# Layer A's attention: output-projection pairs prepared behind the last scores, and gate weights fetched for six products at a time

## The chip, the core and the metric

The kernel runs on one core of a Trainium2 chip. The metric is device microseconds (us) of one execution; lower is better. The time quoted for the kernel before is the median of three runs. Durations of single instructions come from one further execution, taken by the hardware profiler.

## What is computed

A two-layer decoder trunk over 2048 tokens, model width 1024, in float32. Only the first layer, layer A, matters here:

```python
u = rmsnorm(h, norm_a_g[i])
proj = u @ w_in_a[i]
q, k, v, f_logit, gate = jnp.split(proj, [...], axis=-1)
...
o = fox_attention(q, k, v, log_f).reshape(b, s, WIDTH_A)
h = h + (o * jax.nn.silu(gate)) @ w_out_a[i]
```

There are 16 heads of 64 dimensions. `fox_attention` is causal softmax attention whose logits carry a cumulative log forget gate. Layer B (sliding-window attention over shared keys and values) follows and is not touched.

## The kernel before, in words

Every float32 matrix product is made of three products of a high and a low part (high x high, high x low, low x high), so operands are first split: ScalarE (ACT) copies the rounded high part, and VectorE (DVE) or GpSimd (POOL) subtracts it from the original to get the low part.

`attention_a` runs 320 steps: 16 heads, for each four chunks of 512 queries, for each chunk 2, 4, 6 or 8 steps of two 128-key blocks. In a step, TensorE (PE) makes the scores (L975, L976), ACT takes the exponential (L990) and the high part (L993), POOL subtracts for the low part (L994), DVE adds the weights into the running row sums in PSUM (L1003), and three steps later PE multiplies with V (L1018). Beside this, "pieces" for the next head find the row maxima: PE at L927, DVE at L938 and L943, and four small copies per 512 queries (L554) on SyncE's queue (SP). At the end of a chunk DVE folds the sums (L888).

The silu gate's projection, 768 products in 32 units of 24 (L1052), is spread between the steps as filler. For each unit, the weights come in tiles of 512 KB that serve twelve products (L1048), from two buffers with the tag `wr`. The last 48 of the 768 products are kept for after the last scores, when the softmax values still have to come: there the tiles alternate between buffers `st` (four, which held the exponentials) and `wr`. A finished unit goes through DVE, ACT, DVE (L1059 to L1061) and is stored.

The output projection `out_a` then runs over 32 pairs, four chunks of 512 tokens by eight pairs of heads, 24 products a pair (L1221). A pair is loaded by `Pairs.load`: two halves of the attention output, the gate, and reciprocal sums (`gated_load`, five transfers into four 256 KB tiles, L1169 to L1174). `Pairs.prepare` then makes it ready (`gated`): POOL adds the halves (L1184), DVE multiplies by the reciprocals and by the gate (L1185, L1186), ACT copies the high part (L1187), DVE subtracts for the low part (L1188). The first pairs are loaded and prepared inside `attention_a` at steps 284 and 298 (`PREP_AT`), and the load of a third follows the last step. In `out_a`, step `s` loads ahead to pair `s + 5`, prepares pair `s + 2`, splits the output weight of pair `s + 2` (`weight_split`, L131 and L132) and loads that of pair `s + 4` into an `st` buffer (L122).

The order in which an engine gets its instructions is not the program's own: a planner orders them by priority (program order) and by when it reckons that operands and buffers are ready, so that early-ready work may be issued well before the place where it is written. `keep_in_program_order` places an instruction behind the one traced before it on its engine. All transfers here are issued on SP's one queue, in order. At run time each engine takes its instructions strictly in the order so fixed, and waits where an operand is missing.

Of the kernel before, what the change touches and what calls it, by code (L numbers as in the profile page):

```python
# [13 lines left out]
F32R = mybir.dt.float32r  # L14
# [3 lines left out]
ALU = mybir.AluOpType  # L18
# [4 lines left out]
P = 128  # L23
# [3 lines left out]
NDT = D // P  # L27
# [4 lines left out]
CH = 512  # L32
# [9 lines left out]
SUM_LAG = 5  # L42
LOAD_AT = 7

PREP_AT = (284, 298)

RAW_AT = 302

# [44 lines left out]
def f_(ap):  # L93
    return ap.bitcast(F32)


class Pairs:
# [6 lines left out]
        self.loaded = self.ready = 0  # L104

    def load(self, s, tags=("wh", "wl", "wh", "wl")):
        self.tiles[s] = [self.t.sb(tag, [P, CH]) for tag in tags]
        self.t.gated_load(s // NDT, s % NDT, self.tiles[s])
        self.loaded = s + 1

    def prepare(self, s):
        if s % 4 == 0:
            self.Y[s // 4] = self.t.sb("big", [P, 4, 2, CH], F32R)
        self.t.gated(self.y(s), self.tiles.pop(s))
        self.ready = s + 1

    def y(self, s):
# [28 lines left out]
class Trunk:  # L146
# [693 lines left out]
    def attention_a(self, op):  # L840


        nc, tc, d = self.nc, self.tc, self.d
        kbt, qbt = self.sb("big", [P, 2, S], F32R), self.sb("big", [P, 2, S], F32R)
        for i in range(2):
# [6 lines left out]
            out=mask_m[:, -P:], in_=mask_m[:, -P:], pattern=[[-1, P]], compare_op=ALU.is_ge,  # L852
# [40 lines left out]
        def recips(h, c0=0, c1=NCH):  # L893

            nr = (c1 - c0) * NSB
            ps = self.ps("sc", [nr, 32])
            nc.tensor.matmul(
                ps, part[:, h % 2, c0:c1].rearrange("p c b -> p (c b)"), self.fold,
                start=True, stop=True,
            )  # L900
            rc = self.sb("sq", [nr, 32])
            nc.vector.tensor_tensor(rc, ps, roots[:nr, 1 if c0 else 0], ALU.mult)
            nc.vector.reciprocal(rc, rc)
            nc.sync.dma_start(
                out=d["rd"][h, c0 * CH : c1 * CH].rearrange("(b i) -> b i", i=32), in_=rc
            )
# [101 lines left out]
        def values(item):  # L1008
            u, p, ph, pl = item
            h, ch = units[u]  # L1010
            v = heads[h][4]
            if p == 0:
                state[u][1] = self.ps("pa", [P, CH])
            pv = state[u][1]
            last = p == 2 * ch + 1
            for n_, (k, q0, w, off) in enumerate(blocks(ch, p)):
                for i, src in enumerate((ph, pl)):
                    nc.tensor.matmul(  # L1018
                        pv[:, q0 : q0 + w], v[:, k, :], src[:, off : off + w],
                        start=(p == 0 and n_ == 0 and i == 0),  # L1020
                        stop=(last and n_ == 1 and i == 1),
                    )
            if last:
                state.pop(u)
                ov = self.sb("sq", [P, CH])
                nc.scalar.copy(ov, pv)  # L1026
                rows, cols = slice(h * HD, (h + 1) * HD), slice(ch * CH, (ch + 1) * CH)
                nc.sync.dma_start(out=d["om"][rows, cols], in_=ov[:HD, :])
                nc.sync.dma_start(out=d["oc"][rows, cols], in_=ov[HD:, :])

        def gate():


            for ch in range(NCH):
                rows, us = self.factor_rows(0, ch), []
                for dt in range(NDT):
                    us.append([self.sb(t, [P, CH], F32R) for t in ("wh", "wl")])
                    for k in range(2):
                        nc.sync.dma_start(out=f_(us[dt][k]), in_=d["ut"][ch, k, dt])
                for ft in range(NDT):  # L1040
                    if gate_bank == "mx":
                        ps = self.ps("mx", [P, 2, CH])[:, 0]
                    else:
                        ps = self.ps(gate_bank, [P, CH])
                    for dt in range(NDT):
                        if dt % 4 == 0:
                            w = self.sb(next(weight_slots), [P, 2, 2, 2, P], F32R)
                            nc.sync.dma_start(  # L1048
                                out=f_(w), in_=d["wg"][ft, :, dt // 2 : dt // 2 + 2]
                            )  # L1050
                        for i, (wk, uk) in enumerate(((0, 0), (0, 1), (1, 0))):
                            nc.tensor.matmul(  # L1052
                                ps, w[:, dt // 2 % 2, wk, dt % 2, :], us[dt][uk],
                                start=(dt == 0 and i == 0), stop=(dt == NDT - 1 and i == 2),
                            )
                            if dt < NDT - 1 or i < 2:
                                yield
                    g = self.sb("sq", [P, CH])
                    nc.vector.tensor_tensor(g, ps, rows, ALU.mult)  # L1059
                    nc.scalar.activation(g, g, AF.Tanh, scale=0.5)  # L1060
                    nc.vector.scalar_tensor_tensor(g, g, 1.0, ps, ALU.add, ALU.mult)  # L1061
                    nc.sync.dma_start(
                        out=d["gt"][ft * P : (ft + 1) * P, ch * CH : (ch + 1) * CH], in_=g
                    )
                    yield

        pieces, done, loaded = [], 0, 0

        def more_pieces(n):
            nonlocal loaded  # L1070
            while len(pieces) < n and loaded < H:
                load_max(loaded)
                if loaded:
                    load_rest(loaded)
                for ch in range(NCH):
                    pieces.extend(max_pieces(loaded, ch))
                loaded += 1
# [8 lines left out]
        def ahead(target):  # L1086
            nonlocal done
            while done < min(target, len(pieces)):
                pieces[done]()
                done += 1  # L1090
# [6 lines left out]
        yield  # L1097
        pht, plt = self.sb("big", [P, 4, 1024], F32R), self.sb("big", [P, 4, 1024], F32R)
        filler, fed, total = gate(), 0, NCH * NDT * NDT * 3
        gate_bank, weight_slots, rest = "pb", cycle(["wr"]), False  # L1100

        def feed(n, pause=False):


            nonlocal fed, rest
            if pause and rest:
                rest = False
                return
            while fed < min(total, n):
                next(filler, None)  # L1110
                fed += 1
                if pause and fed % (3 * NDT) == 0:
                    rest = True
                    break
# [3 lines left out]
        for n, (u, p) in enumerate(steps):  # L1118
            h, ch = units[u]
            if n % per_head == LOAD_AT and h + 1 < H:  # L1120
                more_pieces(len(pieces) + 1)
            target = per * (n + AHEAD + 1) // per_head + 1
            ahead(target - 1)
            pending.append(scores(n, u, p))
            ahead(target)
            if len(pending) > V_LAG:
                values(pending.pop(0))
            if p == 2 * ch + 1:
                if h == H - 1 and ch in (0, NCH - 1):
                    due.append((n + SUM_LAG, (h, ch and 1, ch + 1)))  # L1130
                elif ch == NCH - 1:
                    due.append((n + SUM_LAG, (h,)))
            while due and due[0][0] <= n:
                recips(*due.pop(0)[1])
            feed((total - KEPT) * (n + 1) // len(steps), pause=True)
            if n == RAW_AT:
                raw = self.sb("big", [P, NDT // 2, D])
                for p in range(NDT // 2):
                    op.weight_load(p, raw[:, p])
            if n in PREP_AT:  # L1140
                op.load(PREP_AT.index(n), ("qn", "wh", "qn", "wl"))
                op.prepare(PREP_AT.index(n))
        op.load(2, ("qn", "wh", "qn", "wl"))
        gate_bank, weight_slots = "mx", cycle(["st", "wr"])
        for item in pending:
            values(item)
            feed(fed + NDT)
        gate_bank = "pb"
        for _, args in due:
            recips(*args)  # L1150
        for p in range(PAIRS_READY):
            op.weight_split(p)
        for _ in filler:
            pass

# [20 lines left out]
                in_=d["rd"][h : h + 1, cols].to_broadcast([HD, CH]),  # L1176
            )

    def gated(self, y, tiles):

        nc = self.nc
        m, c, g, rb = tiles
        yh, yl = (y[:, k] for k in range(2))
        nc.gpsimd.tensor_tensor(m, m, c, ALU.add)  # L1184
        nc.vector.tensor_tensor(m, m, rb, ALU.mult)  # L1185
        nc.vector.tensor_tensor(m, m, g, ALU.mult)  # L1186
        nc.scalar.copy(yh, m)  # L1187
        nc.vector.tensor_tensor(yl, m, f_(yh), ALU.subtract)  # L1188
# [50 lines left out]
    def attention_b(self, w_out, res, dst):  # L1239
# [117 lines left out]
        W = [None, self.half(w_out, 1)]  # L1357
        msg, php, yt = self.sb("big", [P, 4, 1024]), None, None
        load(0)
        load_v(0)  # L1360
        yield
# [176 lines left out]
```

## Time and profile before

| | |
|---|---|
| median of three runs | 2511.83 us (2511.45 to 2513.24) |
| the profiled execution's own time | 2508.55 us |
| its span, first to last instruction | 2506.8 us |
| PE busy | 2455.1 us, 98% of the span |
| DVE busy | 1766.5 us, 70% |
| ACT busy | 1332.5 us, 53% |
| POOL busy | 919.8 us, 37% |
| DMA | 419.30 MB, mean 167 GB/s |

Layer A's attention runs from 594 us, the first scores, to 1484.73 us, the first product of the output projection. Times in rows are microseconds from the span's start. A "busy" PE is not one at its peak: a matrix product counts from its start to its modelled end, and consecutive ones overlap, so PE's rate is better read from how many products a stretch holds and from the granted clock. A bracket at the end of a timeline row gives the engine's idle time just before it and what ended that.

### The profile page before, as it was taken

The page shows a single profiled execution, that of the slowest core. Times are in us where ns is not written, and L with a number is a line of the kernel's source. Part 1 is how long each engine was busy: PE and PEld are TensorE (multiplying, and loading weights), DVE is VectorE, ACT ScalarE, POOL GpSimd, SP SyncE. Part 2 cuts the span into 40 slices and gives each one's busy share as a digit, 9 for nine tenths or more (in the row PEclk, how much of TensorE's full clock was granted, in tenths as well). Part 3 has the DMA queues.
Part 4 walks back from the last instruction along what each step waited for, and adds up shares of the span by engine and source line. Part 5 has one row for each costly group of instructions (what it writes and reads, how often), then busy time and mean ns, then how long its engine had stood idle before and what let it go on. Part 6 is the DMA issues. An engine that isn't in the chain of part 4 may idle for free. (4 is left out here: it accounts for less than half of the span.)

```text
span 2506.8 us, 37302 instructions
## 1 busy us (share of the span) xinstructions
PE 2455.1 (98%) x12256; PEld 2050.1 (82%) x12256; DVE 1766.5 (70%) x4255; ACT 1332.5 (53%) x2574; POOL 919.8 (37%) x611
## 2 busy tenths in 40 slices
PE   8999999999999999999999999999999999899999
PEld 6788899988888777877877778888788888688887
DVE  7656666726888888888888965556666323788885
ACT  5423333415777777877777751145332214777774
POOL 0000000014777777777777752200011000455542
PEclk9999999999999999999999999999999999999999
DMA  5656645687555655565466469965443424755551
GB/s 181 204 158 190 178 148 151 199 268 222 141 149 151 201 142 158 150 186 160 123 202 161 144 186 282 283 216 159 114 131 84 141 91 141 206 168 158 160 143 64
DMA packets 351521, 419.30 MB, mean 167 GB/s; under 512 B 64928, under 2 KB 248256, under 8 KB 345152
## 3 DMA queue, kind: packets, MB, share of 16 engines
q1 hardware_dynamic: 351328, 416.92, 57.3%
q8 instruction: 97, 1.59, 0.3%
q14 instruction: 96, 0.79, 0.1%
HBM read 265.29 MB, written 151.40 MB: 166 GB/s over the span
## 5 line engine op out<-in xcount | busy, mean ns | idle before, releaser
L750 PE MATMUL b<-wh,big 128*128 128x512 f32 (+3 forms) x2560 | 771.6, 375 | 9.2 <-ACT wh L480 8.8
L994 POOL TENSOR_TENSOR big<-st,big 128x1024 fp32r<-128x1024 f32 (+1 forms) x320 | 659.2, 2075 | 276.0 <-ACT big L993 172.0
L750 PEld LDWEIGHTS b<-wh,big 128*128 128x128 f32 x2560 | 472.3, 189 | 80.2 <-ACT wh L480 11.4
L750 PE MATMUL b<-wl,big 128*128 128x512 f32 (+3 forms) x1280 | 474.4, 371 | 1.6 <-DVE wl L481 1.6
L1003 DVE TENSOR_TENSOR ac<-ac,st 128x512 f32<-128x512 f32 (+3 forms) x576 | 355.1, 617 | 53.2 <-ACT st L990 24.5
L990 ACT ACTIVATE st<-sc 128x512 f32<-128x512 f32 (+1 forms) x512 | 274.9, 584 | 158.6 <-PE sc L976 82.5
L1018 PE MATMUL pa<-big 128*128 128x512 f32 (+3 forms) x1280 | 327.1, 370 | 3.2 <-POOL big L994 1.1
L993 ACT CAST big<-st 128x1024 fp32r<-128x1024 f32 (+1 forms) x320 | 295.6, 924 | 7.9
L750 PEld LDWEIGHTS b<-wl,big 128*128 128x128 f32 x1280 | 242.0, 189 | 38.0 <-DVE wl L481 5.5
L1018 PEld LDWEIGHTS pa<-big 128*128 128x128 f32 x1280 | 223.0, 190 | 49.3 <-ACT sq L1026 16.8
L489 ACT ACTIVATE sq<-b,r 128x512 f32<-128x512 f32 (+2 forms) x128 | 77.8, 608 | 302.4 <-PE b L750 299.2
L938 DVE CUSTOM_DVE_ANT_0 mx<-mx,rot 128x128 f32<-128x128 f32 (+3 forms) x240 | 210.5, 877 | 39.3 <-PE mx L927 31.0
L975 PE MATMUL sc<-big 128*128 128x512 f32 (+3 forms) x640 | 231.1, 365 | 1.3 <-DVE st L536 1.1
L976 PE MATMUL sc<-big 67*128 67x512 f32 (+3 forms) x640 | 229.9, 368 | 0.0
L927 PE MATMUL mx<-big 66*128 66x128 f32 (+3 forms) x660 | 192.1, 365 | 11.2 <-DVE mt L938 10.6
L1052 PE MATMUL pb<-wh,wr 128*128 128x512 f32 x488 | 179.3, 399 | 3.8 <-DMA wr<-wg 3.2
L491 DVE TENSOR_REDUCE sm<-sq 128x8 f32<-128x512 f32 (+2 forms) x128 | 74.9, 585 | 139.3 <-ACT sq L489 139.0
L715 PE MATMUL b<-big,wh 128*128 128x512 f32 x512 | 158.3, 390 | 1.4 <-DVE st L721 1.3
L1309 POOL TENSOR_TENSOR st<-st,rs 128x1024 f32<-128x1024 f32 (+1 forms) x64 | 118.4, 1850 | 109.9 <-DVE rs L1308 101.8
L850 POOL MEMSET rot<- 128x1024 bf16 x1 | 1.0, 952 | 421.0 <-PE pb L343 421.0
L927 PEld LDWEIGHTS mx<-big 66*128 66x128 f32 x660 | 113.7, 191 | 50.9 <-DVE mt L938 20.9
L975 PEld LDWEIGHTS sc<-big 128*128 128x128 f32 x640 | 121.6, 190 | 23.1 <-DVE st L536 1.5
(252 smaller groups left out, 4306.4 us busy)
## 6 DMA issues: line engine op xcount, KB each, us to landing
wr<-wg SPq DMA_DIRECT2D x62, 512.0 KB
va<-st SPq DMA_DIRECT2D x32, 512.0 KB
ka<-st SPq DMA_DIRECT2D x64, 256.0 KB
ut<-big SPq DMA_DIRECT2D x16, 1024.0 KB
big<-ka SPq DMA_DIRECT2D x16, 1024.0 KB
big<-qa SPq DMA_DIRECT2D x16, 1024.0 KB
qb<-st SPq DMA_DIRECT2D x64, 256.0 KB
big<-qb SPq DMA_DIRECT2D x16, 1024.0 KB
```

Source lines behind the costliest of these rows:

```text
L715: nc.tensor.matmul(ps, W[k][dt][:, ft * P : (ft + 1) * P], u[ch][:, dt, :], start=(dt == 0 and i == 0), stop=(dt == NDT - 1 and i == 2),)
L750: nc.tensor.matmul(ps[:, :n], u[tb // 4][:, dt, us], W[k][dt], start=(dt == 0 and i == 0), stop=(dt == NDT - 1 and i == 2),)
L927: mm = nc.tensor.matmul(ps[:, b, :wb], qb[:66, i * P : (i + 1) * P], kb[:66, k0 + b * wb : k0 + (b + 1) * wb], start=True, stop=True,)
L938: nc.vector.tensor_tensor_reduce(out=lg, in0=lg, in1=mask, scale=1.0, scalar=NEG, op0=ALU.add, op1=ALU.max, accum_out=f_(o),)
L975: nc.tensor.matmul(o, ka[:, ks], qa[:, qs], start=not (last and n_), stop=False)
L976: nc.tensor.matmul(o, kb[:, ks], qb[:, qs], start=False, stop=not diag)
L990: nc.scalar.activation(pf[:, off : off + w], ps[:, :w], AF.Exp, scale=HD**-0.5)
L993: nc.scalar.copy(ph[:, :tw], pf[:, :tw])
L994: nc.gpsimd.tensor_tensor(pl[:, :tw], pf[:, :tw], f_(ph[:, :tw]), ALU.subtract)
L1003: nc.vector.tensor_tensor(a_, a_, pf[:, off : off + w], ALU.add)
L1018: nc.tensor.matmul(pv[:, q0 : q0 + w], v[:, k, :], src[:, off : off + w], start=(p == 0 and n_ == 0 and i == 0), stop=(last and n_ == 1 an ...
L1052: nc.tensor.matmul(ps, w[:, dt // 2 % 2, wk, dt % 2, :], us[dt][uk], start=(dt == 0 and i == 0), stop=(dt == NDT - 1 and i == 2),)
```

## The change

The pairs' first preparation leaves the score loop. At step 298 pair 0 is only loaded. Behind the last step pair 1 is loaded into two `st` buffers, pair 0 is prepared with its addition (POOL) and first multiplication (DVE) pinned in program order, and pair 2 is loaded into the buffers of pair 0. Pair 1 is prepared, pinned likewise, ahead of the last 24 gate products. The gate weights are fetched in places of 256 KB for six products: four places in the two `wr` buffers during the steps, and four more in two `st` buffers after them.

```diff
-PREP_AT = (284, 298)
+PAIR_AT = 298
...
     def load(self, s, tags=("wh", "wl", "wh", "wl")):
-        self.tiles[s] = [self.t.sb(tag, [P, CH]) for tag in tags]
+        if len(tags) == 4:
+            self.tiles[s] = [self.t.sb(tag, [P, CH]) for tag in tags]
+        else:
+            both = [self.t.sb(tag, [P, 2, CH]) for tag in tags]
+            self.tiles[s] = [t[:, k] for t in both for k in range(2)]
...
-    def prepare(self, s):
+    def prepare(self, s, pin=False):
...
-                        if dt % 4 == 0:
-                            w = self.sb(next(weight_slots), [P, 2, 2, 2, P], F32R)
-                            nc.sync.dma_start(
-                                out=f_(w), in_=d["wg"][ft, :, dt // 2 : dt // 2 + 2]
-                            )
+                        if dt % 2 == 0:
+                            w = next(weight_slots)
+                            nc.sync.dma_start(out=f_(w), in_=d["wg"][ft, :, dt // 2])
...
+        def weight_places(tag):
+            tiles = [self.sb(tag, [P, 2, 2, 2, P], F32R) for _ in range(2)]
+            return [t[:, k] for t in tiles for k in range(2)]
...
-        gate_bank, weight_slots, rest = "pb", cycle(["wr"]), False
+        places = weight_places("wr")
+        gate_bank, weight_slots, rest = "pb", cycle(places), False
...
-            if n in PREP_AT:
-                op.load(PREP_AT.index(n), ("qn", "wh", "qn", "wl"))
-                op.prepare(PREP_AT.index(n))
+            if n == PAIR_AT:
+                op.load(0, ("qn", "wh", "qn", "wl"))
+        gate_bank, weight_slots = "mx", cycle(weight_places("st") + places)
+        op.load(1, ("st", "st"))
+        op.prepare(0, pin=True)
         op.load(2, ("qn", "wh", "qn", "wl"))
-        gate_bank, weight_slots = "mx", cycle(["st", "wr"])
         for item in pending:
             values(item)
             feed(fed + NDT)
...
         for p in range(PAIRS_READY):
             op.weight_split(p)
+        feed(total - 3 * NDT)
+        op.prepare(1, pin=True)
         for _ in filler:
             pass
...
-    def gated(self, y, tiles):
+    def gated(self, y, tiles, pin):
...
-        nc.gpsimd.tensor_tensor(m, m, c, ALU.add)
-        nc.vector.tensor_tensor(m, m, rb, ALU.mult)
+        both = (
+            nc.gpsimd.tensor_tensor(m, m, c, ALU.add),
+            nc.vector.tensor_tensor(m, m, rb, ALU.mult),
+        )
+        for ins in both if pin else ():
+            self.tc.keep_in_program_order(ins)
```

## Rows read from the trace of the kernel before

**Rows 1.** Busy time by stretch, heads 10 to 14; the columns stand first.

```profile
core 0: us, PE busy (x) PEld busy (x) DVE busy (x) ACT busy (x) POOL busy (x), PEclk, DMA share, GB/s
1133.35:1188.47 55.12, 54.27 (x266) 43.59 (x265) 47.21 (x88) 41.58 (x66) 41.08 (x21) 1.00 0.54 153
1188.47:1242.67 54.20, 53.94 (x266) 43.76 (x265) 47.38 (x89) 41.26 (x66) 40.97 (x21) 1.00 0.50 128
1242.67:1300.62 57.95, 54.70 (x267) 43.93 (x266) 47.23 (x89) 41.35 (x67) 41.09 (x21) 1.00 0.67 203
1300.62:1362.96 62.34, 57.99 (x275) 46.14 (x274) 54.92 (x94) 43.72 (x70) 44.65 (x22) 0.97 0.60 158
1362.96:1423.95 60.99, 56.94 (x268) 45.05 (x267) 54.79 (x95) 43.04 (x68) 44.85 (x23) 0.97 0.51 150
```

**Rows 2.** Timeline of DVE: the fold of the sums that ends head 13.

```profile
1362.26 0.70 DVE L888 TRANSPOSE_TENSOR_REDUCE part<-ac 128x16 f32<-128x512 f32 x1
```

**Rows 3.** Timeline of POOL: first and last of four pair additions among the scores.

```profile
1335.04 1.29 POOL L1184 TENSOR_TENSOR qn<-qn,wh 128x512 f32<-128x512 f32 x1 [2.68 <-PE pa L1018]
...
1406.56 1.28 POOL L1184 TENSOR_TENSOR wh<-wh,wl 128x512 f32<-128x512 f32 x1 [1.08 <-DMA wl<-oc]
```

**Rows 4.** Groups of DVE instructions from 1335 to 1416 us; columns first.

```profile
line engine op names shapes xcount | busy us, mean ns | idle before us <-releasers
L1003 DVE TENSOR_TENSOR ac<-ac,st 128x512 f32<-128x512 f32 (+3 forms) x46 | 29.1, 632 | 2.7 <-ACT st L990 1.1 <-ACT ac L997 1.1
...
L1185 DVE TENSOR_TENSOR qn<-qn,wl 128x512 f32<-128x512 f32 x3 | 8.2, 2726 | 2.2 <-POOL qn L1184 1.3 <-DMA wl<-rd 0.8
L1188 DVE TENSOR_TENSOR big<-qn,big 128x512 fp32r<-128x512 f32 x3 | 4.2, 1404 | 0.0
```

**Rows 5.** PE's waits, 1330 to 1420 us (total, times, longest).

```profile
PE mx L927 <- DVE mt L938: 7.6, 4, 2.8
```

**Rows 6.** Timeline of PE behind one such wait: slow products, then fast.

```profile
1407.12 0.63 PE L975 MATMUL sc<-big 128*128 128x512 f32 x1
...
1410.38 0.39 PE L1052 MATMUL pb<-wh,wr 128*128 128x512 f32 x1
```

**Rows 7.** PE's waits, 590 to 1500 us: gate weights not landed.

```profile
PE pb L1052 <- DMA wr<-wg: 3.2, 5, 1.9
```

**Rows 8.** Timeline behind the last scores: POOL, DVE.

```profile
1454.61 18.28 POOL L994 TENSOR_TENSOR big<-st,big 128x1024 fp32r<-128x1024 f32 x8 [1.23 <-ACT big L993]
...
1469.17 2.86 DVE L132 TENSOR_TENSOR big<-big 128x1024 fp32r<-128x1024 f32 x1 [0.94 <-ACT big L131]
...
1473.08 1.21 DVE L132 TENSOR_TENSOR big<-big 128x1024 fp32r<-128x1024 f32 x1
1474.22 0.70 DVE L888 TRANSPOSE_TENSOR_REDUCE part<-ac 128x16 f32<-128x512 f32 x1
```

**Rows 9.** Timeline, one pair from load (SP) through POOL to ready (DVE).

```profile
1481.61 0.38 SPq L1169 DMA_DIRECT2D wh<-om  x1
...
1486.72 1.28 POOL L1184 TENSOR_TENSOR wh<-wh,wl 128x512 f32<-128x512 f32 x1 [13.84 <-DMA wh<-om]
...
1491.24 0.95 DVE L1188 TENSOR_TENSOR big<-wh,big 128x512 fp32r<-128x512 f32 x1 [0.75 <-ACT big L1187]
```

**Rows 10.** Timeline of PE: the output projection begins.

```profile
1484.73 1.52 PE L1221 MATMUL b<-big 128*128 128x512 f32 x6
1487.11 3.04 PE L1221 MATMUL b<-big 128*128 128x512 f32 x12 [0.86 <-DVE sq L1061]
```

**Rows 11.** Busy time by stretch around the seam; columns as in rows 1.

```profile
1470.00:1480.00 10.00, 8.98 (x42) 6.75 (x41) 8.67 (x12) 4.09 (x7) 2.88 (x2) 1.00 0.68 204
...
1500.00:1510.00 10.00, 10.00 (x46) 8.28 (x45) 4.67 (x6) 1.94 (x3) 2.79 (x2) 1.00 1.03 332
```

**Rows 12.** Timeline of DVE: pair 6 ready, then output weight 7 ready.

```profile
1499.44 0.69 DVE L1188 TENSOR_TENSOR big<-wh,big 128x512 fp32r<-128x512 f32 x1 [0.69 <-ACT big L1187]
...
1513.17 1.23 DVE L132 TENSOR_TENSOR big<-st,big 128x1024 fp32r<-128x1024 f32 x1 [0.26 <-ACT big L131]
```

**Rows 13.** SP's own waits, 590 to 1470 us (total, times, longest).

```profile
SPq L1048 <- PE pb L1052: 77.1, 18, 9.8
SPq L554 <- DVE ac L1003: 56.6, 61, 3.3
```

More of the change, by code (lines that the diff above doesn't have):

```diff
@@ L106, in load @@
     def load(self, s, tags=("wh", "wl", "wh", "wl")):
-        self.tiles[s] = [self.t.sb(tag, [P, CH]) for tag in tags]
+        if len(tags) == 4:
[3 more added lines that the diff above has]
+            self.tiles[s] = [t[:, k] for t in both for k in range(2)]
         self.t.gated_load(s // NDT, s % NDT, self.tiles[s])
         self.loaded = s + 1
-    def prepare(self, s):
+    def prepare(self, s, pin=False):
         if s % 4 == 0:
             self.Y[s // 4] = self.t.sb("big", [P, 4, 2, CH], F32R)
-        self.t.gated(self.y(s), self.tiles.pop(s))
+        self.t.gated(self.y(s), self.tiles.pop(s), pin)
         self.ready = s + 1
@@ L1045, in gate @@
                     for dt in range(NDT):
-                        if dt % 4 == 0:
-                            w = self.sb(next(weight_slots), [P, 2, 2, 2, P], F32R)
-                            nc.sync.dma_start(
-                                out=f_(w), in_=d["wg"][ft, :, dt // 2 : dt // 2 + 2]
-                            )
+                        if dt % 2 == 0:
+                            w = next(weight_slots)
+                            nc.sync.dma_start(out=f_(w), in_=d["wg"][ft, :, dt // 2])
                         for i, (wk, uk) in enumerate(((0, 0), (0, 1), (1, 0))):
                             nc.tensor.matmul(
-                                ps, w[:, dt // 2 % 2, wk, dt % 2, :], us[dt][uk],
+                                ps, w[:, wk, dt % 2, :], us[dt][uk],
                                 start=(dt == 0 and i == 0), stop=(dt == NDT - 1 and i == 2),
```

## The prediction

> **What bounds the kernel now.** The page comes first: PE is busy for 98% of the span, so what counts is where PE stands still or is slowed in the stretch that the change touches. I then cut layer A's attention by heads and read the busy times by stretch. The reader should see that a head has a steady price: 55.12 and 54.20 us for heads 10 and 11 [rows 1]; each stretch ends with the fold of the head's last sums, as head 13's at 1362.26 + 0.70 [rows 2]. Head 12 takes 57.95, and heads 13 and 14 take 62.34 and 60.99, with about the same number of products [rows 1]. In these last two DVE's busy time grows from 47 to 55 us, and the granted clock falls from 1.00 to 0.97 [rows 1]. So something is added to DVE there, and PE pays.
>
> The timeline of POOL says what: four pair additions stand among the scores, from 1335 to 1407 us [rows 3]. The program writes only two preparations there. The planner has moved them ahead of their place and has pulled a third pair and half of a fourth in behind them. The groups of DVE show the price. The first multiplication of a pair takes 2.73 us in the mean and the last subtraction 1.40 [rows 4], where the running sums, with one input in PSUM and mostly of the same size, keep 0.63 in the same stretch [rows 4]. Three first multiplications make 8.2 us and also kept DVE idle for 2.2 us before them [rows 4]. DVE takes its work in order, so the maxima and sums queued behind them come late, and PE waits for them four times, 7.6 us in all [rows 5]. Behind such a wait PE's products take 0.63 us instead of 0.39 for over 3 us [rows 6]: the granted clock, whose mean over these heads is 0.97 [rows 1], is at the lower of its two levels, 1.2 instead of 2.4 GHz.
>
> The last view is of the seam between the scores and the output projection, where the removed work must go; its rows come with the steps below.
>
> **The change part by part.**
>
> *Out of the score loop.* No preparation is left among the scores: pair 0 is pinned behind the last of POOL's and DVE's work for them, pair 1 behind pair 0, and pair 2 needs the buffers of pair 0. Heads 13 and 14 should then cost what heads 10 and 11 cost, 54.66 in the mean: 62.34 + 60.99 - 2 x 54.66 = 14.0 us [rows 1]. I count the waits and the slow products inside this sum, not beside it. With head 11 as the measure it would be 14.9; if only the four waits went, 7.6 [rows 5].
>
> *Gate weights in places of six.* A buffer is refilled when its last product is done. With two buffers of twelve, the next fetch has the time of twelve products to land; with four places of six, that of eighteen. PE now waits 3.2 us for such fetches in five waits, the longest 1.9 [rows 7]. Some 45 products go into a head of 54.66 us, 1.2 us each, so the lead grows by 7 us, more than the longest wait. The gain lies between nothing (if the queue ahead of a fetch, and not the free buffer, sets its time) and 3.3 us (all that head 12 takes over heads 10 and 11 [rows 1]). I take 2.0. The number of fetches doubles from 64 (two for each of 32 units) to 128 at half the size; their issue lies on SP, and its price is a rival below.
>
> *Pair 0 behind the last scores.* POOL ends its last subtraction at 1472.89 and DVE folds the last sums at 1474.22 to 1474.92 [rows 8]. The chain of a pair from POOL's addition to the last subtraction, its waits included, took 1492.19 - 1486.72 = 5.5 us [rows 9]. Pair 0, loaded long before, is so ready near 1480.4. The projection starts at 1484.73 [rows 10], under the 48 kept gate products that PE works on meanwhile. So it costs nothing, with 4.3 us of cover; without it, each us late is a us.
>
> *Pair 1.* Its two `st` buffers come free when POOL is done, 1472.9. From issue to ready the pair in [rows 9] took 1492.19 - 1481.61 = 10.6 us, so pair 1 is ready near 1483.6. PE took six products, waited, and went on at 1487.11 [rows 10]; at 46 products in 10 us [rows 11] a pair's 24 take 5.2, so the next pair starts near 1491.0. Cover 7.4 us, cost nothing. What is queued behind its pinned multiplication on DVE is the finishing of the last gate unit, for which PE waits at the start of the projection (0.86 us idle at 1487.11 [rows 10]). DVE's added instructions there are short, 0.69 each [rows 12]; one or two of them before that finishing make 0 to 1.4 us. I take 1.0.
>
> *Pair 2 and the queue behind it.* Its load waits for pair 0's last subtraction, 1480.4; with 10.6 us it is ready at 1491.0 and is wanted at 1496.2. Cover 5.2 us. SP issues in order, so what stands behind this load waits too: the stores of the last values, the following pairs and the output weights 4 to 7.
>
> *The stream of the following pairs.* Pairs 1, 2 and half of pair 3, some 2.6 MB, were loaded among the scores and now come at the seam. At the 332 GB/s of the projection's start [rows 11] that is 7.9 us; from 1473 to 1480 the DMA moved 204 GB/s [rows 11], which leaves room for 0.9 MB or 2.7 us. So the stream comes 5.2 us later. Pair 6 is now ready at 1500.13 and wanted at 1491.0 + 5 x 5.2 = 1517; output weight 7 is ready at 1514.40 and wanted at 1522.2 [rows 12]. The tightest cover, 7.8 us, holds by 2.6. I take nothing, with up to 5 us as the bound.
>
> *The sum.* -14.0 - 2.0 + 1.0 = -15.0 us. The profiled execution took 2508.55, so it becomes 2493.6. The median of the runs before lies 3.3 us above it; the prediction is 2511.8 - 15.0 = 2496.8 us.
>
> **A rule against the trace.** The two-input DVE instructions stretch to 2.73 us beside POOL [rows 4], and the first weight split behind the scores took 2.86 us while POOL still subtracted, the next one 1.21 [rows 8]; the running sums, whose one input is in PSUM, kept 0.63 [rows 4]. The Trainium skill (SBUF — State Buffer, "SBUF: two separate sides") says that a DVE instruction with two SBUF inputs and a GpSimd instruction that reads SBUF exclude each other for a whole instruction, and the trace agrees. It also speaks against the change: the additions of pairs 0 and 1 now fall among the weight splits, and by this rule each can hold DVE for all of its 1.28 us, so the sum by the rule would be 1.6 us worse than mine at most (an estimate from that page: 2 x 1.28 in place of my 1.0). It does not decide anything, since the cover there is larger.
>
> **The rivals.**
>
> *Given back at the projection.* The seam's transfers come late: the stores of the last values and pair 2 hold SP, output weights and pairs follow, and the first pass over eight pairs waits. If pair 2 misses its cover by 3 us and output weight 7 its own by another 3, 6 us go back and the gain is 9: 2502.8 us. For it: DMA is full there, 332 GB/s [rows 11]. Against it: margins of 5.2 and 7.8 us.
>
> *The slow heads stay.* The change does not do what it says: the planner moves other early-ready work, such as weight splits, into heads 13 and 14, or something else makes them slow. Then only the gate weights gain: 2509.8 us. Against it: the swelling of DVE by the pairs accounts for the loss, and the weight splits had a free hand before and came after the last scores [rows 8].
>
> *Slower: SP blocked by twice the fetches.* In the score loop SP stood 77.1 us behind 18 fetches whose buffer was not yet free, and the row maxima's copies go through the same queue [rows 13]. With 128 fetches instead of 64, copies that the next head's scores need can stand behind a fetch, and PE waits for them. It decides from 15.0 / 64 = 0.23 us of added PE wait for each added fetch; at 0.4 us it costs 25.6, and the time is 2522.4 us. For it: one queue in strict order. Against it: the 64 fetches of before cost PE only 3.2 us [rows 7], and the copies' own waits are for DVE and not for fetches [rows 13].
>
> **How the numbers follow.** Forecast 0.76, given back 0.13, slow heads stay 0.05, slower 0.06. About 0.2%, 5.0 us, is what a measurement of this kernel can tell from no change. The forecast's own range: the bounds are -14.9 - 3.3 = -18.2, and -14.0 + 1.4 + 5 = -7.6. The range of 2493.0 to 2504.0 takes in that and the first rival, and leaves out the two others and the end at which the four waits alone go. Faster by more than 0.2%: the forecast and most of the first rival, with a part taken off for heads that recover less, 0.83. Within: 0.10. Slower: 0.07, the third rival and what of the first may go beyond its price.
>
> **What would show it.** Right: no pair addition on POOL before the last subtraction of the scores; heads 13 and 14 at 54 to 56 us with the granted clock at 1.00; DVE busy near 47 us in them; PE's waits for gate weights under 1.5 us; the first product of the projection some 15 us earlier, near 1469; PE without waits over 2 us in its first eight pairs. Wrong: heads 13 and 14 still above 58 us; PE waiting on DVE's L1188 or L132 in the projection by more than 3 us in all; waits of PE for DVE's maxima that stem from copies late on SP.

## The result, and the profile after

The changed kernel takes 2515.43 us (median of 22 runs, 2509.84 to 2519.24); the kernel before, on the same chip, 2510.99 us (22 runs). The ratio is 1.002, interval 1.0014 to 1.0026: slower by some 4.4 us, where 15 us of gain were predicted. The profiled execution took 2515.97 us, its span is 2514.1 us, against 2506.8.

Cut at three points of PE's work, the two spans differ as follows (the last product of the scores is L976 before and L980 now; the 25th and the last product of the projection are L1221 before and L1239 now):

| stretch | before, us | after, us | difference |
|---|---|---|---|
| start to the last product of the scores | 1467.8 | 1462.1 | -5.7 |
| from there to the 25th product of the projection | 23.6 | 34.0 | +10.5 |
| 25th to last product | 169.4 | 170.9 | +1.6 |
| behind the projection | 846.1 | 847.0 | +0.9 |

These sum to +7.3 us for the two profiled executions; the medians differ by 4.4. So the score loop did gain, and the seam behind it lost more. The first cut is from the timeline of PE, before and after; the third line is DVE's last fold now:

```profile
1467.79 0.28 PE L976 MATMUL sc<-big 67*128 67x128 f32 x1
...
1462.10 0.27 PE L980 MATMUL sc<-big 67*128 67x128 f32 x1
...
1463.92 0.72 DVE L892 TRANSPOSE_TENSOR_REDUCE part<-ac 128x16 f32<-128x512 f32 x1
```

That fold comes 10.3 us earlier than before (1474.22 [rows 8]), nearly twice what PE gained. It lay 6.4 us behind PE's last score before and lies 1.8 behind it now. PE's waits show none for it in either kernel, since 51 gate products are still to do, so 4.6 of the 10.3 us are DVE's own. The busy times by stretch, head 13 and head 14 of the kernel after, show the gain:

```profile
core 0: us, PE busy (x) PEld busy (x) DVE busy (x) ACT busy (x) POOL busy (x), PEclk, DMA share, GB/s
...
1301.25:1360.70 59.45, 56.06 (x264) 45.41 (x263) 47.33 (x89) 41.25 (x66) 41.00 (x20) 0.94 0.52 137
1360.70:1417.10 56.40, 55.99 (x273) 45.12 (x273) 48.37 (x89) 43.27 (x69) 41.42 (x21) 1.00 0.53 148
```

Against [rows 1], DVE's busy time is back at 47 to 48 us, as in heads 10 and 11, and no pair addition stands on POOL before the last subtraction. But head 13 still takes 59.45 us, at a clock of 0.94: something new stands there. The groups of PE's waits from 590 to 1700 us (total, times, longest) of the kernel after name it, and the larger one at the seam:

```profile
PE mx L1054 <- DMA st<-wg: 6.2, 1, 6.2
PE pb L1054 <- DMA wr<-wg: 5.8, 4, 3.2
PE mx L931 <- DVE mt L942: 3.7, 16, 0.6
PE b L1239 <- DVE sq L1063: 2.5, 1, 2.5
```

The third line is what [rows 5] were: the waits for maxima fell from a longest of 2.8 to 0.6 us. The second answers to [rows 7]: the waits for gate weights, which the smaller places should have ended, grew from 3.2 to 5.8. The first is new. The timeline of the kernel after shows both places; first head 13, SP and then PE:

```profile
1317.41 0.75 SPq L885 DMA_DIRECT2D big<-va  x1
1318.21 1.79 SPq L1052 DMA_DIRECT2D wr<-wg  x1
...
1325.94 0.77 PE L1054 MATMUL pb<-wh,wr 128*128 128x512 f32 x1 [3.21 <-DMA wr<-wg]
```

The fetch is issued 0.8 us behind the megabyte of the next head's values, and PE gets it 7.7 us later. The kernel before issues the fetch with the same product's weights 6.0 us behind that megabyte, and PE uses it 4.3 us later, without a wait, although it is twice as large; SP and PE of the kernel before:

```profile
1316.64 0.76 SPq L881 DMA_DIRECT2D big<-va  x1
...
1322.63 0.38 SPq L1048 DMA_DIRECT2D wr<-wg  x1
...
1326.90 0.39 PE L1052 MATMUL pb<-wh,wr 128*128 128x512 f32 x1
```

Then the seam, SP, DVE and PE of the kernel after:

```profile
1467.50 0.33 SPq L1181 DMA_DIRECT2D wh<-oc  x1
...
1471.40 0.32 SPq L1182 DMA_DIRECT2D qn<-gt  x1
...
1472.28 1.52 SPq L1052 DMA_DIRECT2D st<-wg  x3
...
1470.68 0.69 DVE L1206 TENSOR_TENSOR big<-qn,big 128x512 fp32r<-128x512 f32 x1 [0.69 <-ACT big L1205]
...
1477.53 0.79 PE L1054 MATMUL mx<-wh,st 128*128 128x512 f32 x1 [6.18 <-DMA st<-wg]
1478.12 0.63 PE L1054 MATMUL mx<-wl,st 128*128 128x512 f32 x1
...
1482.44 0.40 PE L1054 MATMUL mx<-wl,st 128*128 128x512 f32 x1
...
1486.30 1.52 PE L1239 MATMUL b<-big 128*128 128x512 f32 x6
1490.35 4.30 PE L1239 MATMUL b<-big 128*128 128x512 f32 x12 [2.53 <-DVE sq L1063]
```

Read it from SP. Pair 2's load begins at 1467.50, but one of its two `qn` tiles holds pair 0 until DVE's last subtraction, 1470.68 + 0.69. Its gate can so be issued only at 1471.40, and the kept gate products' fetches into `st`, three of them, stand behind it, at 1472.28. PE has run out of weights at 1471.3 and waits 6.18 us; its products then take 0.63 us in place of 0.40, at the lower clock (granted clock 0.50 from 1475 to 1480 us). The last two gate units end together, and PE waits for their finishing, 2.53 us, at the seventh product of the projection. In the kernel before the two `st` fetches were issued at 1466.5 and 1468.9, with no pair's load near them.

### The profile page after: what moved, and what is told of

Its sections match the earlier page's. It is cut to its first block, busy times and chain, and to the rows that moved or that the text cites. A ratio compares the mean times of both kernels' runs of the same rounds, so it can differ in the third digit from the quotient of the medians.

```text
span 2514.1 us, 37443 instructions
## 1 busy us (share of the span) xinstructions
PE 2458.8 (98%) x12256; PEld 2054.6 (82%) x12256; DVE 1757.6 (70%) x4255; ACT 1333.2 (53%) x2574; POOL 917.5 (36%) x611
## 5 line engine op out<-in xcount | busy, mean ns | idle before, releaser
L980 PE MATMUL sc<-big 67*128 67x512 f32 (+3 forms) x640 | 229.6, 368 | 0.0
L1239 PE MATMUL b<-big 128*128 128x512 f32 x576 | 137.8, 392 | 3.5 <-DVE sq L1063 2.5
```

The lines of the kernel that those rows point to most:

```text
L980: nc.tensor.matmul(o, kb[:, ks], qb[:, qs], start=False, stop=not diag)
```

## The experiments

Theory Q: the kept gate products' fetches are late because they stand on SP behind pair 2's load. Rival B: pair 1's load took the first free `st` buffers. Rival F: the fetches of six cost by themselves, in the loop too. All times below are medians beside the kernel before on the same chip; "last score" and "25th" are the two cuts of the table above, in the one profiled execution (before: 1467.8 and 1491.4).

| run | us | before | ratio, interval | last score | 25th | last product | span |
|---|---|---|---|---|---|---|---|
| e1 | 2510.73 | 2509.61 | 1.0001 (0.9992 to 1.001) | 1464.2 | 1495.2 | 1664.5 | 2510.5 |
| e2 | 2510.05 | 2509.61 | 0.9995 (0.9986 to 1.0004) | 1461.9 | 1488.5 | 1658.8 | 2506.6 |
| e3 | 2513.49 | 2509.61 | 1.0014 (1.0005 to 1.0023) | 1458.9 | 1496.1 | 1665.7 | 2513.4 |
| e4 | 2516.73 | 2509.61 | 1.0021 (1.0012 to 1.003) | 1472.8 | 1496.0 | 1665.6 | 2511.6 |
| e5 | 2504.73 | 2508.06 | 0.9989 (0.998 to 0.9999) | 1459.2 | 1485.3 | 1655.3 | 2504.5 |
| e6 | 2507.73 | 2508.06 | 0.9999 (0.9991 to 1.0008) | 1462.2 | 1490.5 | 1662.3 | 2507.4 |
| e8 (one run) | 2514.62 | | | 1472.6 | 1498.6 | 1667.9 | 2512.9 |
| e9 | 2508.01 | 2508.06 | 0.9996 (0.9987 to 1.0005) | 1464.7 | 1488.3 | 1657.6 | 2503.1 |
| e10 | 2506.06 | 2509.47 | 0.999 (0.9981 to 0.9999) | 1457.6 | 1484.7 | 1654.2 | 2505.2 |
| e11 | 2506.03 | 2509.47 | 0.9992 (0.9983 to 1.0) | 1456.2 | 1483.1 | 1653.8 | 2504.3 |
| e12 | 2506.63 | 2509.18 | 0.9987 (0.9978 to 0.9996) | 1458.7 | 1481.2 | 1653.6 | 2502.8 |
| e13 | 2506.44 | 2509.18 | 0.9988 (0.9979 to 0.9996) | 1457.7 | 1480.9 | 1653.5 | 2504.7 |

One execution's cuts can lie some 3 us off: e9, whose median is that of the kernel before, has its last score 3.1 us earlier.

**e1, e2: the loads moved behind the last values.** In e1 `op.load(2)` alone, in e2 `op.load(1)` too:

```diff
-        op.load(1, ("st", "st"))
         op.prepare(0, pin=True)
-        op.load(2, ("qn", "wh", "qn", "wl"))
         for item in pending: ...
+        op.load(1, ("st", "st"))
+        op.load(2, ("qn", "wh", "qn", "wl"))
```

> The changed kernel with one move: pair 2 is loaded behind the pending softmax values instead of ahead of them, so that the gate fetches into `st` stand ahead of it on SP's queue. Theory Q (queue: the fetches were late because they stood behind pair 2's load, which waits for pair 0's last subtraction): the fetches go out between 1464 and 1468 us instead of 1472.3 to 1475.6, PE's wait of 6.2 us for them falls below 2, the slow clock behind it is gone, and the kernel takes 7 to 10 us less than the changed one, near 2505. Theory B (buffers: the fetches were late because pair 1 took the first two `st` buffers, and the fetches get the ones that the last steps free): they cannot go out before 1466, PE still waits 3 us or more, and 3 to 5 us are won. Theory F (the finer fetches themselves cost the time, in the loop and at the seam): no change, near 2515.

> The changed kernel with the loads of pairs 1 and 2 both behind the pending values, so that the four fetches into `st` get the first free buffers and stand ahead of both. Theory Q: as the run with pair 2 alone moved, within 2 us. Theory B: PE does not wait for the fetches at all, and this run is 3 us or more faster than the one with pair 2 alone moved. Theory F: near 2515. If the pairs' own lateness mattered (the rival of the prediction), PE would now wait in the projection for pair 1 or 2 by 2 us or more and this run would be slower than the other.

In e1 the wait for `st` fell from 6.2 to 0.5 us: Q, and pair 1's buffers (B) were not what held them. But the wait at the projection's seventh product grew from 2.5 to 4.7, so part of the gain was handed on: from the last score to the 25th product e1 takes 31.0 us, where the changed kernel takes 34.0. The time lies well above the 2505 that Q expected. In e2, which takes 26.6 us there and whose median is 0.7 us lower, no `st` wait is left; the one fetch that still stood behind the loads, the last into `wr`, cost 3.8 us alone, in the groups of PE's waits of e2:

```profile
PE pb L1054 <- DMA wr<-wg: 9.5, 7, 3.8
```

**e3, e4: the halves of the change alone.** e3 keeps the pairs' part and fetches for twelve products as before; e4 keeps the pairs as before and has the places of six.

```diff
-                        if dt % 2 == 0:
-                            w = next(weight_slots)
-                            nc.sync.dma_start(out=f_(w), in_=d["wg"][ft, :, dt // 2])
+                        if dt % 4 == 0:
+                            w = self.sb(next(weight_slots), [P, 2, 2, 2, P], F32R)
+                            nc.sync.dma_start(
+                                out=f_(w), in_=d["wg"][ft, :, dt // 2 : dt // 2 + 2]
+                            )
...
```

> Only the pairs' part of the change: gate weights in tiles of twelve products as before. Theories Q and B: the score loop gains as in the changed kernel or a little more, heads 13 and 14 near 55 us, and PE waits 5 us or more at the seam for the gate tiles, so the time stays near 2513. Theory F: both losses vanish, and the time is near 2498.

> Only the gate weights' part of the change: places of six products, pairs prepared among the scores as before. Theories Q and B: the seam is as before; PE's waits for gate weights in the loop lie between 2 and 7 us, and the time is within 4 us of before, near 2511. Theory F: slower than before by 5 us or more. The prediction's term for the longer lead wanted 2 us less than before.

e3 has the loop's gain whole: PE's last score comes 8.9 us earlier than before, and head 13 takes 54.8 us, without its wait. And it has the seam's loss, larger (37.2 us from the last score to the 25th product), here with tiles of 512 KB to land. PE's last score and its waits in e3:

```profile
1458.93 0.28 PE L980 MATMUL sc<-big 67*128 67x128 f32 x1
...
PE mx L1056 <- DMA st<-wg: 11.4, 1, 11.4
```

e4 is slower in the loop, its last score 5.0 us later than before. Its head 13 took 68.6 us, where the old one took 62.34 [rows 1]; the timeline of PE in e4 has the same wait at the same place as the changed kernel:

```profile
1325.71 0.77 PE L1050 MATMUL pb<-wh,wr 128*128 128x512 f32 x1 [3.29 <-DMA wr<-wg]
```

So both halves cost, at different places: the places in head 13 (F), the pairs at the seam (Q).

**e5, e6: both loads behind the last gate fetch.** e5 with tiles of twelve, e6 with places of six (there `total - 5`):

```diff
-        op.load(1, ("st", "st"))
         op.prepare(0, pin=True)
-        op.load(2, ("qn", "wh", "qn", "wl"))
...
         feed(total - 3 * NDT)
+        feed(total - 11)
+        op.load(1, ("st", "st"))
+        op.load(2, ("qn", "wh", "qn", "wl"))
         op.prepare(1, pin=True)
```

> Pairs out of the score loop, gate tiles of twelve as before, and the loads of pairs 1 and 2 written behind the last gate fetch, so that on SP's queue all four fetches of the kept products stand ahead of them. Theory Q (what the change lost at the seam it lost because gate fetches stood behind loads that wait): PE waits less than 1 us in all for gate weights between the last scores and the projection, heads 13 and 14 near 55 and 57 us, the last fold near 1461 and the projection's second pair near 1481; the kernel takes 9 to 13 us less than before, 2497 to 2501. A rival (pairs 1 and 2 are now truly late): PE waits for them at the projection's second and third pair, 3 us or more, and the gain is under 6 us.

> The same order with the changed kernel's places of six. Theory Q: the seam without waits over 1 us; only the loop's waits for gate weights stay, 3.2 us at head 13 with the slow clock behind them, so 4 to 7 us more than the run with tiles of twelve, near 2505. If the places cost nothing when the seam is in order, the two runs are equal within 1 us.

No gate fetch is late at the seam in either, and e5 is faster than the kernel before, by 3.3 us, less than the 9 to 13 expected. e6 is 3 us slower than e5 (4 to 7 were expected), and its last score comes 3.0 us later. That is the places' price again: in the four executions with places of six and no pair in the loop (after, e1, e2, e6) the last score stands at 1461.9 to 1464.2, in the six with tiles of twelve (e3, e5, e10 to e13) at 1456.2 to 1459.2.

**e8, e9: why the places cost.** Theory S: a stock of 24 products is not enough when fetches come in sixes. Theory I: which other transfers a fetch falls in with on SP's queue. e8 is e4 with three places in place of four; e9 is the kernel before with tiles of twelve allocated once for all.

```diff
-        places = weight_places("wr")
+        places = weight_places("wr")[:3]
```

> The kernel before with places of six, but three of them in `wr`, so a stock of 18 products instead of 24. Theory S (what counts is the stock that lies in the buffers while SP's queue stands still at a head's end, not how early a place comes free): waits for gate weights appear at most head ends, more than 20 us in all, where the four places have 4.8, and the kernel is 20 us or more slower. Theory I (the late fetch of head 13 is an accident of what stands next to it in the queue): waits stay under 10 us.

> The kernel before with its gate tiles allocated once, like the change's places, but filled by twelve products' weights as before. If it is the size of six that costs (refilling in halves leaves the stock out of step with SP's standstill, so that it runs out at 1322 us and not at 1327), this is as before within 2 us. If it is the allocation once and for all (another planned order), it is slower by 4 us or more, as the run with places of six.

S is refuted: with a stock of 18 the waits for gate weights were 6.2 us in all, none over 1.7, and head 13 had no wait at 1325. e9 is as the kernel before, so allocating once is not what costs. That the late fetch of head 13 is the work of its neighbour on the queue fits e8 and the timelines of head 13; no run moved that neighbour alone, so it is not shown. Nor is it all that the places cost: e8, without that wait, has its last score as late as e4 (1472.6 and 1472.8).

**e10 to e13: what e5 still lost.** From the last score to the 25th product e5 takes 26.1 us, before it was 23.6. In e5 PE waits 2.75 us at the seventh product. Its timeline, DVE and then PE:

```profile
1475.01 0.62 DVE L1206 TENSOR_TENSOR st<-st 128x512 f32<-128x512 f32 x1
1476.31 1.12 DVE L1208 TENSOR_TENSOR big<-st,big 128x512 fp32r<-128x512 f32 x1 [0.69 <-ACT big L1207]
1477.36 0.68 DVE L1063 TENSOR_TENSOR sq<-pb,rows 128x512 f32<-128x512 f32 x1
1478.73 0.69 DVE L1065 SCALAR_TENSOR_TENSOR sq<-sq,pb 128x512 f32<-128x512 f32 x1 [0.70 <-ACT sq L1064]
...
1475.20 1.52 PE L1241 MATMUL b<-big 128*128 128x512 f32 x6
1479.47 4.57 PE L1241 MATMUL b<-big 128*128 128x512 f32 x12 [2.75 <-DVE sq L1065]
```

The last gate unit's finishing (L1063, L1065) stands behind pair 1's chain (L1206, L1208), and DVE idles in front of that. e10 writes pair 1's preparation behind the last gate unit; e11 also puts that unit into another PSUM bank (`pa`).

```diff
-        op.prepare(1, pin=True)
         for _ in filler:
             pass
+        op.prepare(1, pin=True)
```

> Pairs only, loads 1 and 2 behind the last gate fetch, and now pair 1's pinned work behind the last gate unit as well. Theory D (order on DVE): at the projection's start PE waited 2.75 us because the last gate unit's finishing stood on DVE behind pair 1's chain; with the finishing first it begins as soon as the unit's last product is done, some 2 us earlier. PE's wait at the seventh product falls to 0.3 to 1.0 us, the half clock behind it goes or shortens, the 25th product starts 2 to 4 us nearer to the fold than the 24.3 us of the version before, and the time is 2 to 4 us lower, 2501 to 2503, and 5 to 8 below the kernel before. Rival P (pair 1 was better first): the first multiplication of pair 2 now gets in between the instructions of pair 1 on DVE and waits for its row factors, pair 1 is ready some 3 us later and PE waits for it at the 25th product; the sum is within 1 us of the version before, 2504 to 2505.

> As the kernel beside it, with the last gate unit in the PSUM bank of the values instead of its own. Theory B (bank): the seventh product of the projection waits because its bank lies where the last gate unit's lay; another bank, wanted later or earlier in the projection, moves the wait. If the values' bank is wanted later than the seventh product, PE has no wait above 0.5 us before the 25th product and the time is 1 to 2 us below the kernel beside it. If it is wanted at the first product, the wait grows to about 2 us at the first product, and the time is 1 to 2 us above. Without an effect of the bank: same place, same wait.

The wait did not fall as expected of e10: it grew to 3.80 us, and with 3.81 in e11 the bank made no difference. The timeline of DVE in e10 gives the reason:

```profile
1476.78 0.69 DVE L1063 TENSOR_TENSOR sq<-pb,rows 128x512 f32<-128x512 f32 x1 [3.80 <-DMA gt<-sq]
```

DVE was free from 1473.0 on. The unit's result goes to one of two buffers `sq`, and the one in turn still held the unit before, whose store was issued at 1472.53 and released it at 1476.7. The order on DVE was not the bound; the buffer was. e12 (on e10) and e13 (on e5) give the last unit a tile of its own:

```diff
-                    g = self.sb("sq", [P, CH])
+                    g = self.sb("wl" if (ch, ft) == (NCH - 1, NDT - 1) else "sq", [P, CH])
```

> As the kernel with the last gate unit ahead of pair 1, and that unit's product now goes to a tile of its own (one of the buffers of the normed input) in place of one of the two buffers that it shared with the stores. Theory T (buffer behind a store): DVE waited 3.80 us there for the store of the unit before, since its buffer was not free until that had landed; with a tile of its own its first multiplication starts within 0.5 us of the unit's last product, PE's wait at the seventh product falls from 3.80 to 0.5 to 1.2 us, and the time is 2 to 4 us below that kernel, 2502 to 2504. Rival P: pair 1 then is the last to be ready, since pair 2's first multiplication waits ahead of its last subtraction on DVE; PE waits for it 1 to 3 us at the 25th product, and the time stays within 1 us.

> As the version with the pairs alone and both loads behind the last gate fetch, with that tile alone changed: pair 1's first two multiplications stay ahead of the last gate unit on DVE, its last subtraction stands behind that unit's first multiplication. Theory T: PE's wait at the seventh product falls from 2.75 to 0.5 to 1.2 us, the half clock of 3.4 us behind it goes or shortens, pair 1 is not late, and the time is 2 to 4 us below that version, some 6 to 8 below the kernel before (ratio 0.997). Rival C (the finishing chain itself): product, two multiplications and the tanh between them take 2.1 us against the 1.4 us of six products, the wait stays near 2 because DVE is busy with pair 1, and the time is within 1 us of that version.

The wait fell as theory T had it, from 3.80 to 0.81 us in e12, from 2.75 to 1.48 in e13, and no slow products follow; from the last score to the 25th product they take 22.5 and 23.2 us, so the seam costs nothing any more, and the 25th product starts 10 us earlier than before. The time did not fall by the 2 to 4 us expected: both lie where e5 does. In e13 the first eight pairs, which run without a break before, take the gain back: from the 25th to the 193rd product it takes 42.2 us, before 38.1. The busy times by stretch of e13 (columns as above), and from its timeline the split of output weight 7 on DVE:

```profile
1490.00:1500.00 10.00, 10.00 (x46) 8.29 (x45) 4.93 (x7) 2.23 (x3) 2.58 (x2) 1.00 1.02 303
1500.00:1510.00 10.00, 8.75 (x38) 6.55 (x36) 5.53 (x8) 3.14 (x4) 1.29 (x1) 1.00 1.05 334
1510.00:1520.00 10.00, 8.43 (x36) 6.26 (x36) 4.37 (x5) 1.56 (x2) 2.15 (x2) 1.00 1.04 292
```

```profile
1517.39 1.23 DVE L136 TENSOR_TENSOR big<-st,big 128x1024 fp32r<-128x1024 f32 x1 [0.25 <-ACT big L135]
```

The DMA engines are full (share 1.02 to 1.05), and from 1500 us on PE is not. Weight 7 is ready at 1518.6; it was ready at 1514.4 before [rows 12], when the projection began 11 us later. The loads that left the score loop now come in front of the output weights, of which the first of these four is issued at 1488.61, before at 1476.76. Behind the projection, 851.3 us follow its last product in place of 846.1; 2.0 of that is a new wait of PE, in the groups of PE's waits of e13:

```profile
PE b L754 <- DVE big L384: 2.0, 1, 2.0
```

All five versions whose projection ends before 1656 us (e5, e10 to e13) have this wait, 1.7 to 2.0 us, and 849.2 to 851.3 us behind the projection; the nine other executions take 844.9 to 847.8 there. So up to 5 us of the gain are lost where nothing was changed; what causes it was not tried. In e13 the granted clock is also at half for 3.4 us behind that wait, from 1659, and again near 2154 us; the second is in e6 too, which takes only 845.1 us there.

## Why the prediction was wrong

Term by term, in the profiled executions: the loop gave 8.9 us (e3) in place of 14.0, the places of six cost 3.2 where 2.0 were to be gained, the seam cost 10.5 in place of 1.0, and what follows the 25th product cost 2.5 that the working put at nothing. These make up the +7.3 us.

*Out of the score loop, -14.0: the mechanism right, the size too large.* DVE's busy time is back at 47 to 48 us, with no wait for maxima over 0.6 us (0.8 in e3, which has this step alone). But the working cut the heads at DVE's folds, and DVE lagged behind PE there. By the folds e3 gains 13.5 us, and that this is near 14.0 is luck; its last score on PE comes 8.9 us earlier (8.6 to 11.6 in e5 and e10 to e13). Taken from one head's last score to the next, heads 13 and 14 cost 58.5 and 62.2 us before, 11.4 more than heads 10 and 11, and 54.4 and 56.1 in e3.

*Gate weights in places of six, -2.0: wrong sign.* They cost 3.2 us in the changed kernel (last score against e3), 3.0 in e6 (against e5), 5.0 in e4. The gain was there in head 12, 56.1 us where e3 takes 58.2; head 9 (56.2 against 54.6) and head 13 (58.8 against 54.4) lost more. The working took the free buffer as what sets a fetch's time and gave the queue ahead of it only as a reason for no gain. It did not count that the larger number of fetches would be issued at other moments, among other transfers: the one at 1318.21 fell right behind a megabyte. SP's timeline could have warned of it: the kernel before issues no gate fetch from 1290.05 to 1322.63 us, the changed one none from 1291.2 to 1318.21, so the head's end leaves PE on its stock of 24 products in both, and the first fetch behind it must not be slow. Nor did the lead grow by 7 us: that fetch went out 4.4 us sooner, but the plan had its product 4.2 us sooner on PE as well, so from issue to want it had 4.5 us where it had 4.3 before.

*Pair 2 and the queue behind it: the step that failed.* The prediction saw that SP would stand for pair 0's last subtraction, and listed what stands behind: the stores, the following pairs, the output weights. The kept gate products' own fetches were not in the list. In the program they are issued by the filler, inside the loop over the last values, that is behind the line of pair 2's load. The 5.2 us of cover were pair 2's; the fetches had none: PE had weights until 1471.3, and they were issued at 1472.28. The seam lost 10.5 us, the echo in the clock and at the projection's start included; e2, which moves the loads and nothing else, gives 7.4 of them back.

*Pair 0, pair 1: right, at no cost.* Counted from the fold, pair 0 was ready after 7.5 us (the working gives 6.2) and pair 1 after 15.8 (9.4), both later than reckoned; but the projection wanted them after 22.4 and 32.2. In e13, without the seam's waits, pair 1 was ready at 1476.0 and wanted at 1480.9. POOL's addition of pair 1, from 1467.41 to 1468.72, did stretch DVE's multiplication beside it, to 1.76 us at 1467.51, where 0.68 is usual. The Trainium skill (SBUF — State Buffer, "SBUF: two separate sides") says that a DVE instruction with two SBUF inputs and a GpSimd instruction that reads SBUF shut each other out for a whole instruction; the trace agrees. It decided nothing.

*The last gate unit's finishing, +1.0: mis-sized, with another cause.* The wait became 2.5 us. Pair 1, ready at 1479.75, was not in the way: on DVE the last unit's two instructions (1487.80, 1489.51) stood behind the other late unit's and among pair 3's multiplications (1487.14, 1488.41). Where the fetches come in time, e10 and e12 show that the result's buffer, held by a store, sets most of the wait; pair 1's place on DVE makes the difference between 1.48 us in e13 and 0.81 in e12.

*The rivals.* "Given back at the projection" was the nearest in kind, a late transfer on SP's queue, but named pair 2 and output weight 7. The changed kernel never came to that point (from the 25th to the 193rd product it takes 38.3 us, before 38.1); e12 and e13, in which the gate fetches are in time, did, and there weight 7 is late as that rival said. "SP blocked by twice the fetches" did not decide: the places cost 3.2 us, 0.05 us for each of the 64 fetches added, against the 0.23 it needed, and the waits for maxima shrank. "The slow heads stay" fell with the first step. (The forecast's own range ends at -7.6, that is 2504.2 us, just outside the 2504.0 stated.)

**What holds.** Of the 15 us, some 9 to 12 were there to be had in the loop. The version nearest to them is e5 with its successors, 0.1% faster than the kernel before (e12: 0.9987, interval 0.9978 to 0.9996), less than the 0.2% bound of the prediction. The rest is not lost to one wait: take away the fetches' queue and the finishing is late, take that away and the stream of output weights is, and behind the projection up to 5 us go for a reason that stays open.

## What to carry to other kernels

When a load that must wait for a buffer is put into a queue, list every transfer that the program issues later on that queue, those of filler work and of other loops included, and ask of each when its reader runs dry; here the missed one had no cover at all. Work moved out of a loop takes its transfers along: price the stretch that receives them as a stream before counting the gain of the stretch that loses them. A finer grain of fetching is not a longer lead: look at when the queue issues the fetch, what it issues just before, and where the reader stands in its own order. Measure a stretch on the engine that bounds the kernel: DVE's folds showed a gain of 13.5 us where PE's scores came 8.9 earlier.

## What was not expected of the hardware

A gate fetch of half the size landed no sooner when its neighbour was large: 256 KB issued 0.8 us behind a megabyte reached PE 7.7 us after issue, 512 KB issued 6.0 us behind it were in use after 4.3; that the neighbour is the cause was argued and not shown. And a wait of PE costs more than itself: after 6.18 us without weights in the changed kernel, its products started 0.43 us apart in place of 0.23 until 1481.7, and in e3 the granted clock stood at half for 13.7 us around a wait of 11.4.
